# Up weights of the routed experts, split two to three tiles ahead of the matmuls that read them

## The chip, the cores and the metric

The kernel runs on one core of one Trainium2 chip. The metric is the device time of one execution in microseconds; the kernel before took 3189.59 us, the median of three runs (3187.55 to 3194.36).

## The reference, cut to what matters

Two transformer blocks run one after the other on 256 tokens of width 1024. The second ends in a mixture of experts: a router picks 8 of 64 experts for each token, each expert is a gated unit of width 256, and a shared expert sees every token.

```python
sel = lax.top_k(cand, TOP_K)[1]                       # 8 of 64 experts a token
wts = jnp.take_along_axis(scores, sel, axis=1)
wts = wts / jnp.sum(wts, axis=-1, keepdims=True) * ROUTED_SCALE
...
def expert_block(args):
    xe, e = args                                      # xe: rows routed to expert e
    return (jax.nn.silu(xe @ w_gate_l[e]) * (xe @ w_up_l[e])) @ w_down_l[e]
...
routed = jax.ops.segment_sum(yb * slot_w[:, None].astype(yb.dtype), slot_tok, num_segments=t + 1)[:t]
shared = (jax.nn.silu(xt @ w_sh_gate_l) * (xt @ w_sh_up_l)) @ w_sh_down_l
```

All inputs are float32, and every weight is used once in the experts' part, so each of the 64 experts brings 3 MB from memory.

## The kernel before, in words

Every large product is done as three matmuls: each float32 operand x is cut into a high part hi (a rounded copy) and a low part lo = x - hi, and `mm3` adds hi*hi, hi*lo and lo*hi (line 254). To cut a weight tile, `slot` (lines 269 to 288) starts a DMA of 128x1024 float32, 512 KB, from the SyncE queue (SP) into a `raw` tile, lets ScalarE (ACT) write the high part (line 281), and lets VectorE (DVE), or GpSimd (POOL) where it is named, write the low part (line 285). This document calls the three steps together the split of a tile.

The experts' part is `moe`. It takes the experts one by one, and two neighbours that share 128 gathered rows are a pair. The pieces are these:

- `onehot` builds, for four experts, the 0/1 matrices that pick their rows (VectorE), and `gather` multiplies them with the tokens (eight matmuls, then a high and a low part gh, gl).
- `up(e)` multiplies the gathered rows with the gate and up weights of expert e. These come in four tiles, called e.0 to e.3 here, six matmuls each. Then ACT takes the silu and DVE the product with the routing weight (msl).
- `flip(e)` transposes the result and cuts it (mhh, mhl).
- `load(e, f)` splits the two halves of the down weights into tiles xraw, xhi, xlo. Half 0 has its low part made by VectorE, half 1 by GpSimd.
- `down(p)` multiplies a pair's two flipped results with their four down halves, 24 matmuls; `scatter(p)` adds a pair's product to the tokens, one pair later; `slots` prepares the next pair.

The steady order on TensorE is `slots`, `up` of an odd expert, `flip`, `gather`, `up` of the next even expert, `flip`, `gather`, `scatter`, `down`, and so on; two `up` parts stand side by side, and then a stretch without any. In the source the split of tile e.k stands just ahead of its own matmuls.

Buffers: up tiles have four raw buffers and four hi/lo pairs, in two lanes A and B that alternate. So a tile's hi/lo pair is free when the matmuls of the tile four places earlier have run, and its raw buffer when that earlier tile's low part is made. Down tiles have three xraw and four xhi/xlo.

What sets the order: each engine, and SyncE's queue of DMA starts, works through its instructions in order. That order is not the order of the source. A planner that builds the program plays it through with its own costs, and gives an engine next that ready instruction which was traced first; being earlier in the source is a priority, no more. Where `load` says `issue_after(self.dma)`, its DMA start is bound to stand behind the last raw DMA that was traced, which in the kernel before is the one of tile e.1 (half 0) or e.3 (half 1) of the `up` in which it is called:

```python
w = self.tw(I["moegu"][1 + e, k], 2, eng=nc.gpsimd if e < 3 and k == 3 else None)
if k % 2 and pre is not None:
    load(pre, k // 2)
```

So the four DMA starts for the pair of experts 30 and 31 are bound behind raw 31.1, 31.3, 32.1 and 32.3.

Of the kernel before, what the change touches and what calls it, by code (L numbers as in the profile page):

```python
# [28 lines left out]
NE = 64  # L29
# [186 lines left out]
class K:  # L216
# [1445 lines left out]
    def moe(self, hq, xk, xt, g2col):  # L1662

        nc, I, tc = self.nc, self.I, self.tc
        with ExitStack() as es:
# [5 lines left out]
            pool = es.enter_context(tc.tile_pool(name="moe", bufs=1))  # L1671
            npair = NE // 2
            gat, dw, ot, wcs, pgs, hT, py, spt = {}, {}, {}, {}, {}, {}, {}, {}


            i16, p16 = self.t(pool, [P], "i16", F16), self.t(pool, [NT, NE], "p16", F16)
# [45 lines left out]
            def load(e, f):  # L1722
                with tc.issue_after(self.dma):
                    dw[e, f] = self.slot(I["moed"][1 + e, f], pool, nc.gpsimd if f else nc.vector)

            def up(e, pre):
                gh, gl = gat[e // 4][:2]
                ss = slice((e // 2) % 2 * P, (e // 2) % 2 * P + P)
                pg = self.ps()
                for k in range(4):  # L1730
                    w = self.tw(I["moegu"][1 + e, k], 2, eng=nc.gpsimd if e < 3 and k == 3 else None)
                    if k % 2 and pre is not None:
                        load(pre, k // 2)
                    for j in range(2):
                        c = 2 * k + j
                        self.mm3(pg, (gh[:, c, ss], gl[:, c, ss]), (w[0][:, j, :], w[1][:, j, :]), c == 0, c == NC - 1)
                s = self.t(pool, [256], "msl", bufs=2)
                nc.scalar.activation(s, pg[:, 0:256], AF.Silu)
                nc.vector.scalar_tensor_tensor(s, s, wcs[e // 2][:, e % 2:e % 2 + 1], pg[:, 256:], op0=OP.mult, op1=OP.mult)
                pgs[e] = s  # L1740
# [52 lines left out]
            slots(0, self.ps())  # L1793
            onehot(1)
            up(0, None)
            gather(1, 0)
            for e in range(1, NE + 1):
                if e % 2 and e + 1 < NE:

                    spt[e - 1] = self.ps()  # L1800
                    slots((e + 1) // 2, spt[e - 1])
                if e < NE:
                    up(e, e - 1)
                else:
                    load(e - 1, 0)
                    load(e - 1, 1)
                flip(e - 1)

                if e // 4 + 1 < NE // 4:
                    gather(e // 4 + 1, e % 4)  # L1810
                if e % 4 == 2 and e // 4 + 2 < NE // 4:
                    onehot(e // 4 + 2)
                if e % 2:
                    continue
                if e == NE - 4:
                    g2row = self.row_of(pool, g2col, "grow2")
                if e > 2:
                    scatter(e // 2 - 2)
                down(e // 2 - 1)
# [177 lines left out]
```

## Time and profile before

| what | value |
|---|---|
| median of three runs | 3189.59 us |
| the profiled execution, its own time | 3194.2 us |
| its span, first to last instruction | 3192.4 us |
| mean granted TensorE clock | 0.975 |
| experts' part, first gather to last scatter | 2461 to 3175 us of the span |

The durations in this document come from the profiled execution. Its time is the span and 1.8 us around it, and lies 4.6 us over the median of the three runs. Times of rows count from the span's start. PE is TensorE's matmul row, PEld its weight loads; the end of a matmul row is modelled, and matmuls overlap, so the distance from start to start tells how fast they run.

### The profile page before, as it was taken

The numbers are of one execution on the slowest core, as the hardware profiler recorded it, in microseconds if no ns is written. First come the engines' busy times: TensorE is split into PE (matmuls) and PEld (weight loads), VectorE is DVE, ScalarE is ACT, GpSimd is POOL, SyncE is SP. The second block draws the span as 40 slices with busy tenths as digits, with TensorE's granted clock in tenths as the row PEclk, the third lists the DMA queues.
The fourth block names the chain that finished last, engine by engine and source line by source line (L and its number), as shares of the span: only waits on it lengthen the run. The fifth ranks groups of instructions, "written<-read, shape, count | busy, mean of one in ns | idle before, by whom it ended". The sixth has DMA issues, their size and how long they took to land. (4 is left out here: it accounts for less than half of the span.)

```text
span 3192.4 us, 51605 instructions
## 1 busy us (share of the span) xinstructions
PE 3017.8 (95%) x19882; PEld 2710.4 (85%) x19882; DVE 2460.4 (77%) x4140; ACT 1636.2 (51%) x2298; POOL 517.0 (16%) x311
## 2 busy tenths in 40 slices
PE   5999999999999799999999999978998999999997
PEld 5889999998888688999999888878997787777776
DVE  7555998876677776699887767767777888888886
ACT  4554444454544434444445454443344677766675
POOL 2010220000000423122000000012323222222221
PEclk8899999999999899999999999989998999999999
DMA  6335555567788312555556778842232887787875
GB/s 250 104 103 172 172 177 199 194 216 245 235 264 277 123 40 80 179 179 175 199 196 221 249 229 275 264 154 73 93 126 97 286 304 278 285 288 277 293 281 187
DMA packets 181199, 641.80 MB, mean 201 GB/s; under 512 B 20816, under 2 KB 21328, under 8 KB 180304
## 3 DMA queue, kind: packets, MB, share of 16 engines
q1 hardware_dynamic: 175824, 621.64, 57.0%
q0 software_dynamic: 5120, 16.78, 1.3%
q8 instruction: 158, 2.59, 0.3%
q14 instruction: 97, 0.79, 0.1%
HBM read 617.87 MB, written 20.46 MB: 200 GB/s over the span
## 5 line engine op out<-in xcount | busy, mean ns | idle before, releaser
L281 ACT CAST whiB<-rawB 128x1024 fp32r<-128x1024 f32 x433 | 454.1, 1049 | 446.0 <-PE psB L254 171.8
L281 ACT CAST whiA<-rawA 128x1024 fp32r<-128x1024 f32 x423 | 443.5, 1049 | 406.6 <-PE psA L254 159.4
L285 DVE TENSOR_TENSOR wloA<-rawA,whiA 128x1024 fp32r<-128x1024 f32 x390 | 515.1, 1321 | 154.9 <-ACT whiA L281 148.3
L285 DVE TENSOR_TENSOR wloB<-rawB,whiB 128x1024 fp32r<-128x1024 f32 x405 | 507.2, 1252 | 126.7 <-ACT whiB L281 121.9
L285 POOL TENSOR_TENSOR xlo<-xraw,xhi 128x1024 fp32r<-128x1024 f32 x64 | 170.1, 2658 | 520.6 <-ACT xhi L281 510.5
L254 PE MATMUL psA<-hh,whiA 128*128 128x256 f32 x840 | 244.7, 291 | 6.2 <-ACT hh L294 5.7
L254 PE MATMUL psA<-hh,wloA 128*128 128x256 f32 x840 | 243.4, 290 | 7.5 <-POOL wloA L285 6.5
L254 PE MATMUL psA<-hl,whiA 128*128 128x256 f32 x840 | 243.2, 290 | 2.9 <-DVE hl L295 2.9
L254 PE MATMUL psB<-hh,wloB 128*128 128x256 f32 x832 | 238.4, 287 | 4.8 <-DVE wloB L285 4.8
L254 PE MATMUL psB<-hh,whiB 128*128 128x256 f32 x832 | 239.6, 288 | 0.1
L254 PE MATMUL psB<-hl,whiB 128*128 128x256 f32 x832 | 237.7, 286 | 0.0
L254 PE MATMUL acc<-whiA,hh 128*128 128x512 f32 x512 | 199.2, 389 | 0.0
L254 PE MATMUL acc<-wloA,hh 128*128 128x512 f32 x512 | 199.2, 389 | 0.0
L254 PE MATMUL acc<-whiB,hh 128*128 128x512 f32 x512 | 199.2, 389 | 0.0
L254 PE MATMUL acc<-wloB,hh 128*128 128x512 f32 x512 | 199.2, 389 | 0.0
L254 PE MATMUL acc<-whiA,hl 128*128 128x512 f32 x512 | 199.2, 389 | 0.0
L254 PE MATMUL acc<-whiB,hl 128*128 128x512 f32 x512 | 199.2, 389 | 0.0
L285 POOL TENSOR_TENSOR wloB<-rawB,whiB 128x1024 fp32r<-128x1024 f32 x28 | 74.5, 2662 | 739.7 <-ACT whiB L281 739.7
L285 POOL TENSOR_TENSOR wloA<-rawA,whiA 128x1024 fp32r<-128x1024 f32 x33 | 87.3, 2650 | 628.1 <-DVE zlnry L363 348.2
L254 PEld LDWEIGHTS psA<-hh,wloA 128*128 128x128 f32 x840 | 165.3, 197 | 9.0 <-POOL wloA L285 7.3
L254 PEld LDWEIGHTS psA<-hh,whiA 128*128 128x128 f32 x840 | 165.1, 197 | 7.2 <-ACT hh L294 6.5
L254 PEld LDWEIGHTS psA<-hl,whiA 128*128 128x128 f32 x840 | 165.0, 196 | 3.9 <-POOL wloA L285 1.9
(842 smaller groups left out, 8660.6 us busy)
## 6 DMA issues: line engine op xcount, KB each, us to landing
rawA<-in_moegu SPq DMA_DIRECT2D x130, 512.0 KB, 4.7
rawB<-in_moegu SPq DMA_DIRECT2D x130, 512.0 KB, 5.2
rawA<-in_u SPq DMA_DIRECT2D x128, 512.0 KB, 3.4
rawB<-in_u SPq DMA_DIRECT2D x128, 512.0 KB, 3.3
rawA<-in_v SPq DMA_DIRECT2D x128, 512.0 KB, 4.5
rawB<-in_v SPq DMA_DIRECT2D x128, 512.0 KB, 4.5
xraw<-in_moed SPq DMA_DIRECT2D x128, 512.0 KB, 5.9
rawB<-in_wt SPq DMA_DIRECT2D x40, 512.0 KB, 3.2
```

What stands on the lines that cost most here:

```text
L254: self.pe = self.nc.tensor.matmul(out, lhsT, rhs, start=start, stop=stop, skip_group_check=True).ins
L281: self.nc.scalar.copy(hi[:, :n], w[:, :n])
L285: i = (eng or self.nc.vector).tensor_tensor(lo[:, :n], w[:, :n], hi[:, :n].bitcast(F32), op=OP.subtract)
```

## The change

The splits of the up tiles get a running number n = 4e + k over all 64 experts. A function `ahead(n)` traces all splits up to number n that haven't been traced. Before the matmuls of tile number n it is called for n + 2, and after the last matmuls of `up(e)`, ahead of its silu, for tile (e+1).2. Which engine makes which low part stays as it was, and so do buffers, matmuls and transfers. `load` is still called at the same two places, but the last raw DMA traced before it is now the one of a tile two places further.

```diff
+            self.nup = 0
...
+            uw = {}
+
+            def ahead(n):
+
+                while self.nup <= min(n, 4 * NE - 1):
+                    e, k = divmod(self.nup, 4)
+                    uw[e, k] = self.tw(I["moegu"][1 + e, k], 2, eng=nc.gpsimd if e < 3 and k == 3 else None)
+                    self.nup += 1
+
             def up(e, pre):
                 gh, gl = gat[e // 4][:2]
                 ss = slice((e // 2) % 2 * P, (e // 2) % 2 * P + P)
                 pg = self.ps()
                 for k in range(4):
-                    w = self.tw(I["moegu"][1 + e, k], 2, eng=nc.gpsimd if e < 3 and k == 3 else None)
+                    ahead(4 * e + k + 2)
+                    w = uw.pop((e, k))
                     if k % 2 and pre is not None:
                         load(pre, k // 2)
                     for j in range(2):
                         c = 2 * k + j
                         self.mm3(pg, (gh[:, c, ss], gl[:, c, ss]), (w[0][:, j, :], w[1][:, j, :]), c == 0, c == NC - 1)
+                ahead(4 * e + 6)
                 s = self.t(pool, [256], "msl", bufs=2)
```

## Rows read from the trace of the kernel before

**Rows 1.** The page: the chain of work that ended last, shares of the span by engine.
```profile
DVE 0%; DVEq 0%; ACTq 0%; issue 0%; ACT 0%
```

**Rows 2.** Windows: stretch, its length, busy time of PE, PEld, DVE, ACT, POOL, clock, DMA.
```profile
2450.00:2520.00 70.00, 58.42 (x282) 48.44 (x282) 60.81 (x74) 38.88 (x53) 18.70 (x7) 0.89 0.66 233
...
2489.70:2493.40 3.70, 3.70 (x11) 2.85 (x10) 3.67 (x5) 0.00 (x0) 1.68 (x1) 0.54 0.85 278
...
2520.00:3150.00 630.00, 612.04 (x3099) 496.44 (x3099) 529.90 (x592) 445.81 (x602) 154.10 (x58) 1.00 0.80 286
...
2811.80:2816.00 4.20, 4.20 (x25) 3.63 (x24) 3.66 (x6) 4.16 (x6) 1.17 (x1) 1.00 0.23 62
```

**Rows 3.** Waits of PE, 2520 to 3150: total us, times, longest.
```profile
PE psB L254 <- DVE wloB L285: 13.3, 18, 0.8
PE psB L254 <- DVE wloA L285: 3.7, 5, 1.1
```

**Rows 4.** Waits of PE, 2450 to 2520.
```profile
PE psB L254 <- DVE wloA L285: 4.7, 2, 3.8
PE psB L254 <- DVE wloB L285: 2.1, 1, 2.1
```

**Rows 5.** Timeline of PE, 2814 to 2830: start, duration, what, idle before.
```profile
2814.49 0.38 PE L262 MATMUL psA<-cst,msl 128*128 128x128 f32 x2
...
2819.64 0.39 PE L254 MATMUL psB<-whiA,gl 128*128 128x512 f32 x1
2819.87 0.39 PE L254 MATMUL psB<-whiB,gh 128*128 128x512 f32 x1
2821.06 0.50 PE L254 MATMUL psB<-wloB,gh 128*128 128x512 f32 x1 [0.81 <-DVE wloB L285]
2821.40 0.40 PE L254 MATMUL psB<-whiB,gl 128*128 128x512 f32 x1
...
2829.96 0.39 PE L254 MATMUL psA<-xhi,mhh 128*128 128x512 f32 x1
```

**Rows 6.** Timeline of DVE, 2815 to 2821.
```profile
2815.74 2.81 DVE L285 TENSOR_TENSOR wloA<-rawA,whiA 128x1024 fp32r<-128x1024 f32 x1 [0.54 <-ACT whiA L281]
2818.48 0.47 DVE L1739 SCALAR_TENSOR_TENSOR msl<-msl,wc,psB 128x256 f32<-128x256 f32 x1
2818.87 0.41 DVE L295 TENSOR_TENSOR mhl<-psA,mhh 128x256 fp32r<-128x256 f32 x1
2819.20 0.68 DVE L295 TENSOR_TENSOR gl<-psA,gh 128x512 fp32r<-128x512 f32 x1
2819.80 1.21 DVE L285 TENSOR_TENSOR wloB<-rawB,whiB 128x1024 fp32r<-128x1024 f32 x1
```

**Rows 7.** Groups by form, DVE, 2520 to 3150: count, busy us, mean ns, idle before.
```profile
L285 DVE TENSOR_TENSOR wloA<-rawA,whiA 128x1024 fp32r<-128x1024 f32 x115 | 168.4, 1464 | 20.2 <-ACT whiA L281 18.9
```

**Rows 8.** Timeline of POOL, 2814 to 2818.
```profile
2814.83 2.64 POOL L285 TENSOR_TENSOR xlo<-xraw,xhi 128x1024 fp32r<-128x1024 f32 x1 [5.10 <-ACT xhi L281]
```

**Rows 9.** Timeline of ACT, 2813 to 2817.
```profile
2813.70 1.05 ACT L281 CAST xhi<-xraw 128x1024 fp32r<-128x1024 f32 x1
2814.65 1.06 ACT L281 CAST whiA<-rawA 128x1024 fp32r<-128x1024 f32 x1
...
2816.13 1.06 ACT L281 CAST whiB<-rawB 128x1024 fp32r<-128x1024 f32 x1
```

**Rows 10.** Timeline of SP's DMA starts, 2801 to 2816.
```profile
2801.18 0.33 SPq L266 DMA_DIRECT2D rawB<-in_moegu  x1
...
2805.06 0.33 SPq L266 DMA_DIRECT2D rawB<-in_moegu  x1
2807.14 0.33 SPq L279 DMA_DIRECT2D xraw<-in_moed  x1
...
2815.23 0.33 SPq L266 DMA_DIRECT2D rawB<-in_moegu  x1
```

**Rows 11.** The down weights' tensor: time from DMA start to landing.
```profile
DMA to landing us min/median/max: 3.1/5.9/8.5
```

## The prediction, as it was put on record

> **What bounds the kernel now.** I read the chain of waits first, and it says nothing here: all its shares round to 0% [rows 1], since it follows the end of the program back for some microseconds only. So I read the experts' stretch from the windows. Between 2520 and 3150, TensorE is busy in 612 of 630 us at a granted clock of 1.00; VectorE is busy in 530 (84%), ScalarE in 446 (71%), and the DMA engines have a share of 0.80 [rows 2]. TensorE is the bound, and nearly without a hole. What is left to win stands in its waits, read next: 13.3 us in 18 waits for wloB and 3.7 us in 5 for wloA, both low parts of up tiles [rows 3]. At the start (2450 to 2520) there are 6.8 us in three such waits [rows 4].
>
> A wait costs more than its idle time, because a matmul row is longer than the distance to the next. In the timeline the steady distance is 0.23 us (2819.64 to 2819.87). The matmul on wloB of tile 32.3 starts at 2821.06, 1.19 after its forerunner, so it is 0.96 late where the row shows 0.81 idle; the next start comes after 0.34 instead of 0.23 [rows 5]. That is 0.26 above the idle time for each wait. In the steady stretch: 17.0 + 23 x 0.26 = 23.0 us. At the start: 6.8 + 3 x 0.26 = 7.6 us, and behind the 3.8 us wait TensorE runs 3.7 us at a mean clock of 0.54 [rows 2], near the lower of its two levels (1.2 of 2.4 GHz), which costs 3.7 x 0.46 = 1.7 us. The pool that the change can reach is 23.0 + 7.6 + 1.7 = 32.3 us.
>
> Why is wlo 32.3 late? Follow VectorE back [rows 6]. The low part of 32.3 starts at 2819.80, behind msl, mhl and gl, and these behind wlo 32.2, which took 2.81 us instead of 1.21. It began at 2815.74 while GpSimd's xlo ran from 2814.83 to 2817.47 [rows 8], and it ended at 2818.55, 1.1 after GpSimd: about its whole own time. So VectorE stood still for 1.6 us behind GpSimd. Over the stretch wloA averages 1464 ns in 115 pieces [rows 7]; against 1.21 that is 115 x 0.25 = 29 us of standing still, about one microsecond for each of some 29 pairs, which is the size of the wait. The wait is thus the sum of a late start (the hi/lo pair of 32.2 and 32.3 is free only as the matmuls of 31.2 and 31.3 end, the last by 2814.49 [rows 5]), a collision, and three short products in front.
>
> **The change, part by part.**
>
> *Matmuls, casts, differences, transfers:* none added, none removed. 256 splits keep their engines and durations.
>
> *Priority of the splits.* Number n goes two tiles up in the source, the third tile of the next expert in front of silu, flip and gather. But the fourth tile, e.3, is traced within up(e) before e.1's matmuls, so it still stands behind msl and mhl of the experts before and behind gl. And four hi/lo pairs remain four: ScalarE's cast of 32.2 ran at 2814.65 and that of 32.3 at 2816.13 [rows 9], 1.6 us after its buffer's matmuls at the latest. So most of this priority can't be cashed in: the old plan has already put the casts about where buffers allow. Lower end: 0. Upper end: wlo 32.3 before msl, mhl and gl, that is 2819.80 - 2818.48 = 1.3 us earlier, more than the 0.96 lost, so all of it. I take little of this by itself for the steady stretch; it counts at the start, below.
>
> *DMA starts of the down weights.* This I take for the greater part. `load` is bound behind the last raw DMA traced, now two tiles further. For the pair 30/31 the four starts go from behind raw 31.1, 31.3, 32.1, 32.3 to behind 31.3, 32.1, 32.3, 33.1. The last one started at 2807.14 and can now start only after raw 33.1, that is after 2815.23 + 0.33 [rows 10]. With a landing of 3.1 to 8.5 us, median 5.9 [rows 11], ScalarE's cast of 1.05 [rows 9] and GpSimd's 2.64 [rows 8], GpSimd works from about 2815.6 + 5.9 + 1.05 = 2822.5 to 2825.2, instead of 2814.83 to 2817.47. The collision leaves tile 32.2, which has no slack, for tiles of 33, whose matmuls come behind the down part. Wlo 32.2 then takes 1.21: 1.6 us less in the queue before 32.3, against 0.96 late.
>
> What comes back: the start before it moves from behind 2801.18 to behind 2805.06 [rows 10], 3.9 us later, so VectorE's xlo of expert 31's half 0 (1.2 us) drops from the down part to the place in front of wlo 32.0. That takes up to 1.2 of the 1.6 us away if VectorE has no hole there; it has one of 0.54 [rows 6]. The gain for 32.3 is thus between 1.6 - 1.2 + 0.54 = 0.9 and 1.6 us, against 0.96 needed. It just suffices. Because it is that near I take three quarters of the steady pool: 23.0 x 0.75 = 17.2 us.
>
> *The start.* The 3.8 us wait is for tile 2.2, whose low part now stands before msl, flip and gather of its neighbours; the GpSimd splits of e < 3 stay and collide as before. Ends: 0 and 7.6 + 1.7 = 9.3. I take a third, 3.1 us, since two of three waits lie in a run of collisions that no priority ends.
>
> *Cover.* If the steady stretch shrinks by 23 us, VectorE's share becomes 530/607 = 87% and the DMA share 0.80 x 630/607 = 0.83, both short of the whole. The DMA engines have a hole between 2811.8 and 2816, share 0.23 [rows 2], into which the moved start falls; so it costs nothing there. Without this cover it would queue behind five raw transfers and land near 8.5 us.
>
> Sum: 17.2 + 3.1 = 20.3 us off the profiled execution's 3194.2 us (a span of 3192.4 and 1.8 around it) gives 3173.9. The median of the runs lies 4.6 under that execution, so I predict 3169.
>
> **Rivals.**
>
> *All waits go.* If the priority also puts wlo e.3 before gl, the whole pool of 32.3 us is won: 3189.6 - 32.3 = 3157. For it: VectorE has 16% left. Against: the tile e.3 is not moved past msl and gl.
>
> *The collision only changes its place.* GpSimd has 58 xlo in the stretch, one for each expert, and each must fall somewhere within two `up` parts and a down part. If the planner's account of landing differs from the chip's, the moved one falls on the next even tile, or the other half's on 32.0. Then each pair loses the same microsecond: gain 0 to 6 us, 3184 to 3190. For it: every long wloA costs about 1.6 us wherever it falls. The Trainium skill, "SBUF — State Buffer", section "Who interferes with whom", speaks against the change here: a VectorE instruction with two inputs in SBUF and a GpSimd instruction that reads SBUF exclude each other, and whichever issues first holds the other up for its whole length. By that rule splits moved into the part where GpSimd works would be held up too, and the time would be that of this rival; rows 6 and 8 agree with the rule (2.81 against 1.21).
>
> *Slower: the down part waits for its last half.* One mechanism: the last down half starts 8.4 us later (2807.14 to 2815.6), and its first matmul stands at 2829.96 [rows 5]. At the median landing its low part is done at 2825.2, 4.8 us before; at the longest, 2815.6 + 8.5 + 1.05 + 2.64 = 2827.8, still 2.2 before. It decides from the point where ScalarE's queue (casts of 33.x that wait for their own DMA) or SP's queue adds more than that. If each of some 31 down parts then waits 1.5 us, that is 46 us; less 20 won, the time is 3189.6 + 26 = 3216. Against it: up to 4.8 us of slack.
>
> **How the numbers follow.** Forecast (3160 to 3181, middle 3169): 0.50. All waits go (3152 to 3160): 0.14. Only its place (3181 to 3193): 0.22. Slower (3196 to 3230): 0.14. A measurement of this kernel tells about 0.2%, 6.4 us, from no change. Faster by more (under 3183.2) is the first two and a fifth of the third, less a little for the forecast's own error: 0.66. Within: 0.19. Slower: 0.15. The range that leaves out no more than two in ten runs from 3153, all waits gone, to 3194, the upper end of the third.
>
> **What would show it.** Right: PE's waits for wloB and wloA in the steady stretch fall from 17.0 to some 4 us; GpSimd's second xlo of a pair starts about 8 us later against the `slots` matmuls; wlo of even experts' third tile takes 1.21; long wlo stand on odd experts. The priority alone, without the moved starts, would change little. Wrong: waits of PE for xlo or xhi in the down part; wloA as long as before on even tiles; a DMA share over 0.9 with ScalarE waiting for raw tiles; or a start at tile 2.2 as late as now.

## The result, and the profile after

The changed kernel takes 3214.99 us (median of four runs, 3213.64 to 3216.8) against 3190.62 (four runs): ratio 1.0074 [1.0061, 1.0087], 24.4 us slower, where 3169 was forecast and 3194 was the end of the range. Its profiled execution took 3213.64 us (span 3211.8, granted clock 0.974), 19.4 more than that of before.

Put the two traces side by side at the first `up` matmul of an expert. The changed kernel is 4.1 us ahead at experts 8 and 12, and then 2.3 behind at 20, 9.1 at 32, 14.0 at 40, 17.8 at 52, 19.4 at 63 and at the end. So the start was won, and from expert 12 to 63 nearly a microsecond is lost with each pair on the mean: (19.4 + 4.1) / 25.5 pairs = 0.92 us. The windows of the kernel after (columns as in [rows 2]) show it: at the start TensorE gets 300 matmuls done instead of 282, in the steady stretch 2982 instead of 3099, with every other engine and the DMA share lower too, so no engine and no transfer became the bound.

```profile
2450.00:2520.00 70.00, 61.33 (x300) 50.97 (x299) 59.06 (x76) 40.63 (x55) 17.78 (x7) 0.89 0.66 239
2520.00:3150.00 630.00, 593.55 (x2982) 482.37 (x2981) 510.46 (x575) 433.05 (x581) 137.50 (x55) 0.99 0.77 276
2837.50:2841.00 3.50, 3.50 (x10) 2.70 (x9) 2.54 (x3) 1.41 (x2) 0.00 (x0) 0.53 0.99 386
```

TensorE's waits from 2520 to 3150 after the change (total us, times, longest), to be held against [rows 3]:

```profile
PE psB L254 <- DVE msl L1751: 33.5, 24, 2.3
PE psB L254 <- DVE wloB L285: 2.9, 8, 0.7
```

The waits that the change was to end fell from 17.0 to 2.9 us. A new one of 33.5 us stands in their place. It was there before, as a row too small to look at, and I left it out of the rows:

```profile
PE psB L254 <- DVE msl L1739: 0.7, 3, 0.4
```

Where does a matmul wait for msl? In `down`. Its second column half goes into the accumulator buffer psB that `up` of the even expert has filled (the buffers of a lane are used in turn), so the fourth matmul of `down` must wait until msl has read that buffer out. In the timeline of PE after the change (start, duration, what, idle before) `up` of expert 32 ends and `flip` begins at 2830.92; gather, scatter and the first three matmuls of `down` fill 3.7 us; the fourth should start at 2834.64 and starts at 2836.81:

```profile
2830.92 0.38 PE L262 MATMUL psA<-cst,msl 128*128 128x128 f32 x2
...
2834.41 0.39 PE L254 MATMUL psA<-xhi,mhl 128*128 128x512 f32 x1
2836.81 0.50 PE L254 MATMUL psB<-xhi,mhh 128*128 128x512 f32 x1 [2.01 <-DVE msl L1751]
...
2837.79 0.63 PE L254 MATMUL psA<-xhi,mhh 128*128 128x512 f32 x1
2838.22 0.63 PE L254 MATMUL psA<-xlo,mhh 128*128 128x512 f32 x1
```

So msl has under 4 us from the end of `up`. Why does it take longer? Read back through the queues of the same stretch. First DVE: msl stands behind the low part of tile 33.2, which took 2.31 us instead of 1.21 (the collision with GpSimd). Tile 32.2, which the prediction was about, is clean at 2824.80:

```profile
2824.80 1.21 DVE L285 TENSOR_TENSOR wloA<-rawA,whiA 128x1024 fp32r<-128x1024 f32 x1
...
2834.05 2.31 DVE L285 TENSOR_TENSOR wloA<-rawA,whiA 128x1024 fp32r<-128x1024 f32 x1 [1.37 <-ACT whiA L281]
2836.28 0.47 DVE L1751 SCALAR_TENSOR_TENSOR msl<-msl,wc,psB 128x256 f32<-128x256 f32 x1
```

GpSimd's low part of the last down half lies right beside it:

```profile
2832.88 2.40 POOL L285 TENSOR_TENSOR xlo<-xraw,xhi 128x1024 fp32r<-128x1024 f32 x1 [10.22 <-ACT xhi L281]
```

And DVE itself waited for ACT, whose queue shows three casts one behind the other, each waiting for its transfer, and the silu of expert 32 behind them. It starts 3.0 us after `up` ended:

```profile
2829.77 1.05 ACT L281 CAST whiB<-rawB 128x1024 fp32r<-128x1024 f32 x1 [1.58 <-DMA rawB<-in_moegu]
2831.75 1.05 ACT L281 CAST xhi<-xraw 128x1024 fp32r<-128x1024 f32 x1 [0.93 <-DMA xraw<-in_moed]
2832.97 1.05 ACT L281 CAST whiA<-rawA 128x1024 fp32r<-128x1024 f32 x1 [0.17 <-DMA rawA<-in_moegu]
2833.92 0.38 ACT L1750 ACTIVATE msl<-psB 128x256 f32<-128x256 f32 x1
```

The transfers come from SP's queue, where the last down half's start now stands between raw 33.1 and raw 33.2; from 2824.9 to 2833 the share of the DMA engines is 0.91:

```profile
2824.90 0.33 SPq L266 DMA_DIRECT2D rawB<-in_moegu  x1
2825.28 0.43 SPq L279 DMA_DIRECT2D xraw<-in_moed  x1
2826.04 0.33 SPq L266 DMA_DIRECT2D rawA<-in_moegu  x1
```

Before the change a down half's start stood at this place too (half 0 of expert 32, at 2815.61), but its cast came behind the silu, and raw 33.2 landed 5.0 us after its start instead of 6.8 (in the median of 23 pairs 4.1 instead of 5.7). The low part of 33.2 stood ahead of msl as well, but it ran clean:

```profile
2824.72 1.23 DVE L285 TENSOR_TENSOR wloA<-rawA,whiA 128x1024 fp32r<-128x1024 f32 x1 [0.83 <-ACT whiA L281]
2825.86 0.48 DVE L1739 SCALAR_TENSOR_TENSOR msl<-msl,wc,psB 128x256 f32<-128x256 f32 x1
```

The silu ahead of it on ACT:

```profile
2824.59 0.37 ACT L1738 ACTIVATE msl<-psB 128x256 f32<-128x256 f32 x1
```

There `up` ended at 2822.34, the silu started 2.25 us later, and TensorE's row on msl came at 2826.39 with 0.18 us idle: nothing was to spare. So in this pair the wait grew by 1.83 us, 0.75 of it from the later silu and 1.08 from the collision (2.31 - 1.23). Over the 27 even experts from 6 to 58, counted from the start of the last matmul of `up`, the silu starts after 1.20 us before the change and 2.55 after it, and msl ends after 2.85 and 5.17: of the 2.3 us, ACT's queue has rather more than half.

The account of the 23.5 us lost in the steady stretch: waits (33.5 + 2.9) - (13.3 + 3.7 + 0.7) = 18.7; six more of them at 0.26 each, 1.6; about 3 are left. Matmuls at the lower clock, as behind the wait shown (last row of the windows: 0.53 from 2837.5 to 2841), are of that size: over the stretch the granted clock is 0.99 instead of 1.00. How much of the 3 us they are was not taken apart.

### The profile page after: what moved, and what is told of

It reads as the page before. It is cut to its first block, busy times and chain, and to the rows that moved or that the text cites. A ratio compares the mean times of both kernels' runs of the same rounds, so it can differ in the third digit from the quotient of the medians.

```text
span 3211.8 us, 51604 instructions
## 1 busy us (share of the span) xinstructions
PE 3018.9 (94%) x19882; PEld 2713.2 (84%) x19882; DVE 2456.2 (76%) x4140; ACT 1640.2 (51%) x2298; POOL 503.1 (16%) x311
## 5 line engine op out<-in xcount | busy, mean ns | idle before, releaser
L285 POOL TENSOR_TENSOR xlo<-xraw,xhi 128x1024 fp32r<-128x1024 f32 x64 | 159.3, 2489 | 548.1 <-ACT xhi L281 492.3
L281 ACT CAST xhi<-xraw 128x1024 fp32r<-128x1024 f32 x128 | 134.6, 1051 | 71.1 <-PE psB L254 39.5
```

What stands on the lines that cost most here:

```text
L281: self.nc.scalar.copy(hi[:, :n], w[:, :n])
L285: i = (eng or self.nc.vector).tensor_tensor(lo[:, :n], w[:, :n], hi[:, :n].bitcast(F32), op=OP.subtract)
```

## The experiments

The theory (A): the moved DMA starts of `load` put the second down half's cast and its collision in front of silu and msl of the even expert, and `down` waits for the accumulator buffer. Rivals: (B) the priority of the splits does it, by putting the low part of (e+1).2 ahead of msl; (C) the buffer order of `down` is at fault and the rest would be a gain; (D) the collision with GpSimd costs the same wherever it is put. Each kernel is the changed one with the edit shown, except where a line says otherwise. The wait rows are TensorE's from 2520 to 3150.

One thing about the bindings must be known first. A binding only says behind which raw DMA a start has to stand; other raw DMAs that are traced ahead of it can still go in between. So binding a start as before does not always put it where it was. This is the raw DMA that each start of a pair really stands right behind, read from SP's queue for the experts 10 to 55 (e is the start's own expert):

| kernel | even e, half 0 | even e, half 1 | odd e, half 0 | odd e, half 1 |
|---|---|---|---|---|
| before | (e+1).1 | (e+1).3 | (e+1).1 | (e+1).3 |
| changed, and those not named below | (e+1).3 | (e+2).1 | (e+1).3 | (e+2).1 |
| both halves bound as before | (e+1).1 or (e+1).2 | (e+2).1 | (e+1).3 | (e+1).3 |
| the same, silu and msl in front | (e+1).1 | (e+2).1 | (e+1).3 | (e+1).3 |
| half 1 bound as before | (e+1).3 | (e+2).1 | (e+1).3 | (e+1).3 |
| half 0 bound as before | (e+1).2, in 2 of 23 (e+1).3 | (e+2).1 | (e+1).3 | (e+2).1 |
| half 1's cast behind the silu | (e+1).3 | (e+2).2 | (e+1).3 | (e+2).2 |
| before, without GpSimd | (e+1).2 | (e+1).3 | (e+1).1 | (e+1).3 |

### Each half of the change alone

Meant as the priority alone: `ahead` keeps the raw DMA of each tile in `ud`, and the starts are bound to the same ones as before. By the table only two of the four come back, the even expert's half 0 and the odd expert's half 1:

```diff
-            def load(e, f):
-                with tc.issue_after(self.dma):
+            def load(e, f, after=None):
+                with tc.issue_after(after or self.dma):
...
+                    ud[e, k] = self.dma
...
-                        load(pre, k // 2)
+                        load(pre, k // 2, ud[e, k])
```

> The changed kernel, but the DMA starts of the down weights stand behind the same raw DMAs as before the change (tile e.1 and e.3 of the running up part); only the priority of the splits is left of the change. Theory (the moved DMA starts make it slow: the last down half lands between the raw tiles of the next odd expert, ScalarE casts it in front of the silu of the even expert, its GpSimd part collides with the low part in front of msl, and the down part's second bank waits for msl): PE's waits for msl fall from 34.4 us to under 5, the waits for wloB come back to about 17 us, and the time is that of before, 3185 to 3197. Rival (the splits' priority puts casts and low parts in front of silu and msl): the waits for msl stay near 34 us and the time near 3215.

Binding alone: the kernel before, in which `ahead` traces only the raw DMAs two tiles ahead, the casts and low parts not:

```diff
+                    ur[e, k] = self.raw(I["moegu"][1 + e, k])
...
-                    w = self.tw(I["moegu"][1 + e, k], 2, eng=nc.gpsimd if e < 3 and k == 3 else None)
+                    ahead(4 * e + k + 2)
+                    w = self.tw(None, 2, eng=nc.gpsimd if e < 3 and k == 3 else None, raw=ur.pop((e, k)))
...
+                ahead(4 * e + 6)
```

> The kernel before, but the raw DMAs of the up tiles are traced two tiles earlier, so that the DMA starts of the down weights stand behind the raw DMA of a tile two places further, as in the changed kernel; casts and low parts of the up tiles stay where they were in the source. Theory (moved DMA starts): as slow as the changed kernel, 3208 to 3222, with PE's waits for msl over 25 us. Rival (priority of the splits): 3185 to 3195, waits for msl about 1 us.

Measured: priority with the starts bound as before 3195.67 us, 1.0016 [1.0006, 1.0025]; binding alone 3209.54, 1.0057 [1.0036, 1.0078]. In differences of medians (the kernel before beside them: 3190.48) that is 5 and 19 us. That they add up to the 24 of the change says nothing, since two moved starts are in both. The wait for msl comes with the binding:

```profile
PE psB L254 <- DVE msl L1749: 29.4, 23, 2.4
PE psB L254 <- DVE wloA L285: 3.3, 8, 0.8
```

With the priority and two starts put back it stays small, and the old wait grows:

```profile
PE psB L254 <- DVE wloB L285: 26.5, 21, 2.2
PE psB L254 <- DVE msl L1752: 1.0, 4, 0.4
```

The groups of DVE say why (the same kernel; count, busy us, mean ns): the long low parts are now those of lane B, 26 of 27 on the even experts' fourth tile, while wloA is nearly clean. In [rows 7] it was wloA, with 17 of 18 long ones on the even experts' third tile.

```profile
L285 DVE TENSOR_TENSOR wloB<-rawB,whiB 128x1024 fp32r<-128x1024 f32 x113 | 162.8, 1441 | 4.0 <-ACT whiB L281 3.2
L285 DVE TENSOR_TENSOR wloA<-rawA,whiA 128x1024 fp32r<-128x1024 f32 x114 | 143.4, 1258 | 28.1 <-ACT whiA L281 27.7
```

B falls as the main cause: the moved starts bring the wait for msl and 19 of the 24 us with every cast traced where it was. The priority with all four starts as before was not run.

### Another order in `down`

All of the first column half first, so that psB is needed after 12 matmuls, not after 3:

```diff
-                for z in range(2):
-                    e = 2 * p + z
-                    for f in range(2):
...
-                        for q in range(2):
+                for q in range(2):
...
+                    for z in range(2):
+                        e = 2 * p + z
+                        for f in range(2):
...
```

> The changed kernel, but the down part does all 12 matmuls of its first bank before the 12 of its second, instead of 3 and 3 in turn; so the first matmul on the second bank, the one that waits for msl, comes 9 matmuls (2.0 us) later. Nothing is left out. If the wait for msl is what costs (34.4 us in 25 waits of 1.4 us, the longest 2.3), nearly all of it goes: waits for msl under 4 us, time 3215 - 34 to 40 = 3175 to 3183, faster than both kernels. Rival (TensorE is short of something else, DMA or VectorE, and waits at the next place instead): 3205 to 3220, with waits moved to other tiles.

Measured 3195.29 us, 1.0020 [1.0008, 1.0032]. The wait for the buffer is gone, 20 us are back, but the time that I expected is missed by 12: mhl of the pair's odd expert, which stands in DVE's queue behind msl of the next even one, is now needed within the second six matmuls instead of the second twelve, and is the next to be late.

```profile
PE psA L254 <- DVE mhl L295: 16.1, 18, 1.4
PE psB L254 <- DVE wloB L285: 5.2, 8, 1.0
PE psB L254 <- DVE msl L1751: 0.7, 1, 0.7
```

So C holds for the wait alone. The lateness sits in the queues of ACT and DVE.

### Silu and msl in front

The split of (e+1).2 is bound behind silu and msl of expert e:

```diff
-                ahead(4 * e + 6)
...
-                nc.scalar.activation(s, pg[:, 0:256], AF.Silu)
-                nc.vector.scalar_tensor_tensor(s, s, wcs[e // 2][:, e % 2:e % 2 + 1], pg[:, 256:], op0=OP.mult, op1=OP.mult)
+                a = nc.scalar.activation(s, pg[:, 0:256], AF.Silu).ins
+                m = nc.vector.scalar_tensor_tensor(s, s, wcs[e // 2][:, e % 2:e % 2 + 1], pg[:, 256:], op0=OP.mult, op1=OP.mult).ins
...
+                with tc.issue_after(a), tc.issue_after(m):
+                    ahead(4 * e + 6)
```

> The changed kernel, but the split of the next expert's third tile is traced behind silu and msl, its cast bound behind the silu on ScalarE and its low part behind msl on VectorE. The moved DMA starts stay. If low part and cast of that tile in front of msl are the larger part of the delay: waits for msl from 34.4 us to under 10, time 3180 to 3192. If the cast of the down half, which still stands in front of the silu, makes the delay: waits for msl stay over 20 us, time 3200 to 3215.

Measured 3185.08 us, 0.9985 [0.9973, 0.9996]. The wait for msl is gone but for one of 0.2 us, and 0.4 us is left in 24 pairs for the tile e.3:

```profile
PE psB L254 <- DVE wloB L285: 9.1, 24, 0.4
PE psB L254 <- DVE wloA L285: 3.6, 12, 0.9
```

The same with the starts bound as before (the edit of the first experiment on top):

> The kernel with silu and msl in front of the next expert's third tile (e5), and with the DMA starts of the down weights bound where they were before the change. If the delay of msl was the one harm of the moved starts, e5 has already removed it, and going back changes little: 3180 to 3190, waits for msl under 2 us. Rival (the moved starts also help, because they take GpSimd's collision off the even experts' third tile, as the prediction had it): waits for wloA and wloB rise from 16.7 us to over 25 and the time to 3190 to 3200.

Measured 3226.5 us, 1.0117 [1.0098, 1.0136], beyond either expectation. So the moved starts are not simply bad: with silu in front the two that went back are worth 41 us. In the pair that I followed, GpSimd's piece (2826.76 to 2829.47) now falls on a small product of `onehot`, which takes 2.16 us instead of 0.68, ahead of the low part of 32.2:

```profile
2827.86 2.16 DVE L1689 TENSOR_TENSOR O<-Oeq,Oeq 128x512 fp32r<-128x512 f16 x1 [0.27 <-PE psA L254]
2829.94 1.21 DVE L285 TENSOR_TENSOR wloA<-rawA,whiA 128x1024 fp32r<-128x1024 f32 x1
```

TensorE waits for the even experts' third tile again. Of those 23 waits, 11 have this long product right ahead of the tile's low part and 8 a low part of half 0 (3.42 to 3.44 us instead of 1.21); the tile itself is long in 2 only.

```profile
PE psB L254 <- DVE wloA L285: 29.6, 23, 2.7
PE psB L254 <- DVE wloB L285: 12.0, 24, 1.5
```

Next, the 0.4 us for the tile e.3. On top of silu in front, the split of (e+1).3 is traced there too, ahead of flip and gather:

```diff
-                    ahead(4 * e + 6)
+                    ahead(4 * e + 7)
```

> As e5, and the next expert's fourth tile is traced at the same place as its third, so in front of flip's and gather's low parts (mhl, gl), which stood before it until now. In e5 the fourth tile of even experts still costs 24 waits of 0.4 us. If mhl and gl in front of it are the cause: waits for wloB fall from 9.8 to under 3 us, time 3172 to 3182. Rival (the buffer that comes free only with the last matmuls of the expert before is the cause, or mhl now comes late for the down part): 3183 to 3195, with waits for mhl or wloB of 8 us or more.

Measured 3170.04 us, 0.9934 [0.9915, 0.9954]: what the change was forecast to bring. Its greatest waits:

```profile
PE psA L254 <- DVE mhl L295: 2.5, 2, 1.7
PE psB L254 <- DVE wloA L285: 2.2, 5, 0.6
```

### Which down half

Half 1 (GpSimd's) bound as before, half 0 as after the change; and the other way round (`k == 1` in this line; `ud` keeps the raw DMAs as above). By the table the first edit puts back the odd expert's half 1 alone; the second moves only the even expert's half 0, by one raw DMA, and so does not set the two halves apart:

```diff
-                        load(pre, k // 2)
+                        load(pre, k // 2, ud[e, k] if k == 3 else None)
```

> The changed kernel, with the DMA start of half 1 of the down weights (the one whose low part GpSimd makes) bound where it was before the change, and that of half 0 left where the change has it. Theory (half 1 of the odd expert is what is cast in front of the silu of the even one and what GpSimd then works on during the low part in front of msl): waits for msl fall from 34.4 to under 8 us, time 3190 to 3200. Rival (half 0, whose low part VectorE makes, is the harm): waits stay over 25 us, time over 3208.

> The changed kernel, with the DMA start of half 0 bound where it was before the change and that of half 1 left where the change has it; the counterpart of e7. Theory (half 1's moved start is the harm): waits for msl stay over 25 us and waits for wloB stay under 6 us, time 3208 to 3220. Rival (it takes both): waits for msl under 15 us.

Measured: half 1 bound as before 3203.45 us, 1.0045 [1.0032, 1.0058]; half 0 bound as before 3202.41, one run and so without an interval. Half 1 bound as before:

```profile
PE psB L254 <- DVE wloB L285: 27.4, 17, 2.2
PE psB L254 <- DVE msl L1752: 3.9, 10, 0.8
```

Half 0 bound as before:

```profile
PE psB L254 <- DVE msl L1752: 32.7, 25, 2.4
PE psB L254 <- DVE wloB L285: 1.4, 2, 0.8
```

The wait for msl belongs to the odd expert's half 1, as A says: this start is the only one that the first edit moves, and the wait falls from 33.5 to 3.9 us. But the wait for wloB comes in its place, with 17 long low parts on the even experts' fourth tile, and the kernel stays 14 us behind the one before. Why the second edit brings 12 us was not followed; its waits do not show it.

Then half 1's DMA start bound as after the change, but its cast, and with it GpSimd's piece, bound behind the silu (`load` takes it as a third argument):

```diff
-                    if k % 2 and pre is not None:
-                        load(pre, k // 2)
+                    if k == 1 and pre is not None:
+                        load(pre, 0)
+                    mark = self.dma
...
-                nc.scalar.activation(s, pg[:, 0:256], AF.Silu)
+                a = nc.scalar.activation(s, pg[:, 0:256], AF.Silu).ins
+                if pre is not None:
+                    last, self.dma = self.dma, mark
+                    load(pre, 1, a)
+                    self.dma = last
```

> The changed kernel; the DMA starts stay where the change has them, but ScalarE's cast of half 1 is bound behind the silu of the running expert, and with it GpSimd's low part comes later. The third tile's split stays in front of the silu. If cast and collision make the delay: waits for msl fall from 34.4 us to under 10, time 3180 to 3195. If the later landing of the third tile's raw data alone suffices (0.75 us of 2.2 in the pair looked at): waits for msl stay over 15 us, time over 3198.

Measured 3169.66 us, 0.9937 [0.9913, 0.9961], more than I expected of it: 45 us off the changed kernel. More than the cast has moved, though: traced later, half 1's start now stands behind the third tile's raw DMA and no longer ahead of it, so the gain belongs to cast, GpSimd's piece and start together.

```profile
PE psB L254 <- DVE msl L1758: 8.2, 5, 2.0
```

Both good edits together (half 1's cast behind the silu; two tiles behind silu and msl), in which half 1's start stands ahead of the third tile's raw DMA again:

> e8 and e9 together: silu and msl in front of the next expert's third and fourth tile, the cast of half 1 behind the silu, DMA starts where the change has them. e8 and e9 each gave 3170. If they remove different waits (e8 those for wlo and msl, e9 those for msl and wlo, each with a few left): under 3168. If they remove the same ones: 3166 to 3174, no better than either.

Measured 3242.85 us, 1.0164 [1.0147, 1.0181], the slowest of all, and a plain miss. Half of all low parts of lane A (53 of 106) are long now, on both experts of a pair; the mean is 2048 ns:

```profile
L285 DVE TENSOR_TENSOR wloA<-rawA,whiA 128x1024 fp32r<-128x1024 f32 x106 | 217.1, 2048 | 47.9 <-ACT whiA L281 47.8
```

In a pair looked at, the two casts now follow each other on ACT right behind the silu (xhi at 2833.36, whiA at 2834.30), so GpSimd's piece starts at 2834.48 and DVE's wloA at 2835.38, for 2.90 us. All 53 pieces of GpSimd in the stretch meet a wloA, and TensorE waits for it and for the mhl that stands behind it:

```profile
PE psB L254 <- DVE wloA L285: 26.5, 27, 1.2
PE psA L254 <- DVE mhl L295: 26.2, 25, 1.3
```

### No GpSimd in the pairs

If the place of a collision decides, its absence must make before and after equal. Half 1's low part goes to DVE, bound behind msl: 60 pieces of 1.22 us more for DVE in the steady stretch (`m` is msl's instruction, `low` makes the low part that `load` leaves out for half 1).

```diff
...
+                    if f:
...
+                        nc.scalar.copy(hi, w)
+                        dw[e, f] = hi, lo, w
...
+            def low(e, m):
+                hi, lo, w = dw[e, 1]
+                with tc.issue_after(m):
+                    nc.vector.tensor_tensor(lo, w, hi.bitcast(F32), op=OP.subtract)
...
+                if pre is not None:
+                    low(pre, m)
```

In the changed kernel:

> The changed kernel, with the low part of half 1 of the down weights made by VectorE behind msl, and none by GpSimd: no collision is left in the steady stretch, but ScalarE's cast of half 1 stays in front of the third tile's cast and the silu, and VectorE has 64 more low parts of 1.2 us. If the collision is the larger part of the delay of msl (1.1 of 2.2 us in the pair looked at): waits for msl fall from 34.4 us to under 12 and no wloA is over 1.3 us; time 3180 to 3200, since VectorE's added work may open other waits. If ScalarE's cast and the late landing are the larger part: waits for msl stay over 20 us, time over 3205.

In the kernel before:

> The kernel before, with the low part of half 1 of the down weights made by VectorE behind msl, as in e11, and none by GpSimd. e11 (the same on the changed kernel) gave 3163.65, 0.9916 of before. If all of that gain is the missing collision: 3160 to 3170 here too, so the change itself is worth nothing without GpSimd. If the change carries part of it (its earlier splits take effect once the collisions are gone): 3172 to 3190 here, with waits for wloB over 8 us.

Measured: 3163.65 us, 0.9916 [0.9899, 0.9932], in the changed kernel; 3164.50, 0.9918 [0.9902, 0.9935], in the one before. Equal, and the two lowest medians of all, though their intervals just overlap those of the two kernels at 3170. In the changed kernel without GpSimd no wloA is long (mean 1222 ns), and the wait for msl shrinks from 33.5 to 4.6 us, although the casts of the down half and of an odd expert's third tile still stand ahead of the silu in ACT's queue. Over the same 27 even experts the silu now starts 1.87 us behind the last matmul's start and msl ends 3.93 behind it, where `down` needs the buffer after some 3.95 (2834.64 against 2830.69 in the pair above): without the collision the later casts alone hardly pass what there is to spare. Its group, its waits and its window:

```profile
L285 DVE TENSOR_TENSOR wloA<-rawA,whiA 128x1024 fp32r<-128x1024 f32 x116 | 141.8, 1222 | 48.0 <-ACT whiA L281 46.3
```

```profile
PE psB L254 <- DVE msl L1765: 4.6, 8, 1.3
PE psB L254 <- DVE wloB L285: 1.5, 2, 1.3
```

```profile
2520.00:3150.00 630.00, 623.19 (x3168) 511.87 (x3167) 552.60 (x662) 455.43 (x612) 0.00 (x0) 1.00 0.82 288
```

The waits of the kernel before, without GpSimd:

```profile
PE psB L254 <- DVE wloB L285: 6.4, 6, 1.8
PE psB L254 <- DVE msl L1753: 0.7, 1, 0.7
```

DVE takes over 60 x 1.22 = 73 us of work and is busy only 552.6 - 529.9 = 22.7 us longer [rows 2]: some 55 us of its busy time before was standing still (the time of its instructions above the median of the same instruction in the two kernels without GpSimd). The change by itself is then worth nothing (3163.65 against 3164.50); what it did was to choose where GpSimd's pieces fall. D falls: with the collisions left in, the same pieces of GpSimd give anything from 3170 to 3243.

## Why the prediction was wrong, step by step

- **What bounds the kernel.** Right: TensorE with some 32 us of holes, of which the two kernels without GpSimd won 26.
- **The wait's cause.** Right: a collision on 32.2 in front of 32.3. But the 29 us of standing still were not about one microsecond in each of some 29 pairs: 18 wloA are long, by 1.57 us each, and in ten other places the collision fell on a product of `onehot` (2.17 to 2.90 us instead of 0.68). And the row of 0.7 us on msl was passed over. Small as it was, three waits of up to 0.4 us said that this path had no slack.
- **Priority.** "Most of this priority can't be cashed in" is right, but not that its lower end is 0. With two of the four starts put back the priority costs 5 us, since the collisions go from the even experts' third tile to their fourth (mean 1441 ns), the tile with nothing to spare. What it does with all four put back is not known.
- **DMA starts of the down weights.** Here it failed. The times were right: GpSimd works at 2832.88, which is 2823.8 after taking off the 9.1 us by which this kernel is late there, against 2822.5 forecast; wlo 32.2 takes 1.21; the waits for wlo fall to 2.9, some 4 forecast. The sentence that failed is the next: "the collision leaves tile 32.2, which has no slack, for tiles of 33, whose matmuls come behind the down part". I asked when the matmuls of 33 come, and not what stands behind its low part in DVE's queue: msl of expert 32, and behind msl the buffer of `down`, due 3.7 us after `up` ends. Its term, 17.2 us won in the steady stretch, came out as 23.5 lost, by the run of the binding alone (19 us) mostly through these starts. The signs that were to show it right came: the waits for wlo went, GpSimd's piece came 9 us later, wlo 32.2 took 1.21, and 27 of 41 long low parts stand on the odd experts' third tile. Not one of them looked at msl.
- **What comes back.** xlo of half 0 was to stand in front of wlo 32.0; it runs at 2825.93, between 32.2 and 32.3. It is not free there: it stands in DVE's queue ahead of the low part of 32.3, for which TensorE still waits 0.39 us in this pair, at 2829.66, one of the 8 waits for wloB that are left.
- **The start.** Right in size: the waits fell from 6.8 to 3.9 us, and the changed kernel is 4.1 us ahead at expert 8, 0.5 of it from before the experts (forecast 3.1). But the wait for tile 2.2 stayed, at 3.7, which was named as a sign of being wrong; the 2.1 for a wloB went. These are the waits from 2450 to 2520, to be held against [rows 4]:

```profile
PE psB L254 <- DVE wloA L285: 3.7, 1, 3.7
PE psB L254 <- DVE wloB L285: 0.2, 1, 0.2
```

- **Cover.** Wrong, and already by the rows: the hole ends at 2816, and the start was forecast for 2815.6, so its transfer runs behind the hole, where the share before the change is 0.90 (2816 to 2822). After the change it lands 6.4 us after its start, between raw 33.1 and 33.2, and ACT waits 1.58, 0.93 and 0.17 us on these three in a row, with the silu behind them. The mean share of the stretch, 0.77, hid this.
- **Rivals.** The slower one named 3216, and 3215 came, but that is chance: TensorE waits for no xhi and no xlo on account of the last down half. The nearest in mechanism was "the collision only changes its place". It was priced at 3184 to 3190, because I held each place to be equally dear. The rule of the Trainium skill that stood beside it ("SBUF — State Buffer", section "Who interferes with whom": the two engines lock each other out for a whole instruction) is borne out: all 40 wloA of over 1.3 us (of 111, mean 1536 ns) overlap a piece of GpSimd, and without GpSimd none is that long. It gives the length of a collision, not its price. Counted as above, the lock took some 55 us of DVE's time before and 49 after, and the kernel with less of it is slower.

What stays open: what the priority does by itself; how much TensorE would wait for msl by ACT's queue alone and by the collision alone, since the kernel without GpSimd has an earlier silu too; and why the planner puts GpSimd's pieces where it does in each kernel. That the two good edits together give 3243 because every piece then meets a wloA is read from the trace; no run tests it.

## What to carry to other kernels

When a transfer or a piece of work is moved, write down for each engine that it passes what is queued behind it, the small instructions that only give a buffer back above all, and when that buffer is needed again; the moved work's own user is only one of those who wait. A wait of a few tenths that turns up in one of ten rounds of a loop marks a path without slack, and it is the first candidate for the next bound. Where two engines lock each other out, count the standing still in both before splitting work between them: here 64 pieces given back to the busier engine gained 26 us, at least as much as the best reordering (20).

## What the runs showed that was not expected

- The time depends on the place of the collisions and not on their sum alone. Counted as above, DVE stands still for 55 us before the change (3190 us), 49 after it (3215), 44 with half 0 bound as before (3202) and 59 with silu and msl in front (3185). The extremes do go with the sum: 42 us in each of the two kernels at 3170, 88 in the one at 3243. With two tiles behind silu, wloA still averages 1547 ns, with half 1's cast behind silu wloB 1497; in both the long ones stand where hardly anything waits, and the kernels are some 6 us behind those with none.
- Behind the wait of 2.01 us TensorE ran at a granted clock of 0.53 for 3.5 us, close to the lower of its two levels (1.2 of 2.4 GHz); matmuls then started 0.43 apart instead of 0.23 (2837.79, 2838.22). Before the change the wait at this place was 0.18 us.
- A start that was bound as before the change did not go back to its old place in two of four cases, since raw DMAs that had been traced earlier went ahead of it in SP's queue. What such an edit does is read from the queue and not from the edit.
